# Gathering an attention chunk's loads into four transfers of ScalarE's queue, one step ahead

## The chip, the cores and the metric

The kernel runs on one core of a Trainium2 chip. Its time is the device time of one execution in microseconds (us), as the median of several runs.

## What is computed

One decoder block on 2048 positions of width 1024, in float32. A normalised input goes through one projection whose columns feed two mixers: a gated linear attention with four heads, and a gated short convolution. Their results go through an output projection, are added to the input, and a SwiGLU feed-forward block and a last norm follow. Cut to the part that matters here:

```python
h = rmsnorm(x, norm1_g)
p_q, p_k, p_v, p_g, p_a, c_b, c_c, c_h = split(h @ w_in)
log_a = log_sigmoid(p_a @ w_gate_up + b_gate) / 16
# per chunk: b = cumsum(log_a)
q_i, k_i, k_s = q * exp(b), k * exp(-b), k * exp(b_last - b)
o = tril(q_i @ k_i.T) @ v + q_i @ state
state = exp(b_last) * state + k_s.T @ v
o = rmsnorm(o, gla_norm_g) * silu(p_g)
```

## The kernel before

All wide products run as seven products of quarter matrices (PRODUCTS, a Strassen scheme), each of them as three matmuls of split operands (`product_step`, L323 to L330: high by high, high by low, low by high). A function `unit` (L332) does one such group: it loads raw weights, splits each quarter with ScalarE and VectorE into one of four `wq` buffers (`split`, L145 to L147), and runs the seven products, 12 matmuls each in the input projection. Between products results leave PSUM by a copy of ScalarE (L348) or an addition of VectorE (L352). The first product's bank is copied out before the third product goes on in the same bank.

The positions are worked through in two halves of two blocks of 512 (`in_proj`, L536). In each half the input projection has twelve units; the first six give k, q, v and the silu of g, and each result of 128 rows by 512 positions is stored to DRAM scratch: `s_kq` (four buffers a block), `s_v` and `s_g` (four each). The forget gate (L507) makes the cumulated decays and stores them to `s_d` (two buffers a block, L532). Every load and store goes through the helpers `load` (L138) and `store` (L141), both on the queue of SyncE, which issues in order.

The attention is background work. `gla_half` (L578) is a generator over eight chunks of 128 positions (two blocks of four), and `tick` (L187), called after each product, lets it go on by a step on every second call. The chunks of the first half run beside the units of both input projections, those of the second half beside the second input projection and the first output projection (L712). A chunk goes through four functions:

- `gla_load` (L603) takes four buffers of 128 by 4 by 128, issues 14 loads of 128 rows by 128 positions (four of k and q, two of the decays, four of v, four of g), and right behind them the two exponentials on ScalarE (L609, L610) and the two scalings of q and k on VectorE (L611, L612).
- `gla_scores` (L617) has TensorE form the scores (L622) and transpose k (L628) and v (L631); ScalarE copies the transposes back (L632, L633) and scales the carried state (L638).
- `gla_outputs` (L641) forms the outputs (L646, L648) and the chunk's state update (L653), and the sums of squares on ScalarE (L670).
- `gla_finish` (L678) transposes, multiplies by the gate and stores to `s_gla` (L686).

All buffers made by `bt` (L134) are of one pool of 11; there are four `wq` buffers, 28 operand pairs `op` and 8 PSUM banks. A scheduler orders each engine's instructions when the program is built, from its own estimate of their times; the engines then run their instructions in that order. Each DMA adds to one of eight completion semaphores, taken in turn, and waits, on the queue that issues it, for the DMA before it on the same semaphore.

The operand pairs of the second half are loaded (`load_pairs`, L476) while the first half's last unit runs: 28 transfers of 512 KB. Those of the output projection are loaded by `build_mix` (L706).

Of the kernel before, what the change touches and what calls it, by code (L numbers as in the profile page):

```python
# [10 lines left out]
F32 = mybir.dt.float32  # L11
# [7 lines left out]
P = 128  # L19
D = 1024  # L20
SEQ = 2048
PB = 512
NB = SEQ // PB
# [24 lines left out]
def tile_hymba_block(ctx, tc, x, xt, win, wa, wgu, wout, wffn, wdown, wdown_first, small, out):  # L48
    nc = tc.nc
    act, dve, pool, pe = nc.scalar, nc.vector, nc.gpsimd, nc.tensor  # L50

    def pool_of(name, bufs, **kw):
        return ctx.enter_context(tc.tile_pool(name=name, bufs=bufs, **kw))
# [8 lines left out]
    dram = pool_of("dram", 1, space=DRAM)  # L62
# [34 lines left out]
    def scratch(name, n):  # L97
        return [
            [dram.tile([P, PB], F32, name=f"{name}{b}_{i}") for i in range(n)] for b in range(NB)
        ]  # L100

    s_kq, s_d, s_v, s_g = scratch("sk", 4), scratch("sd", 2), scratch("sv", 4), scratch("sg", 4)
    s_x1 = scratch("sx", KD)
    s_mix = [[dram.tile([P, 2, PB], F32, name=f"sm{b}_{k}") for k in range(4)] for b in range(NB)]
    s_gla = [dram.tile([P, HEADS, 2, PB], F32, name=f"sgla{b}") for b in range(NB)]
# [19 lines left out]
    def col(c):  # L125
        return sml[:, c : c + 1]

    def bank(name="mm"):
        return ps.tile([P, PB], F32, name=name, tag="mm")

    def tt(name):
        return tp.tile([P, PB], F32, name=name, tag="t")

    def bt(name, shape=(P, PB)):  # L134
        return bx[0].tile(list(shape), F32, name=name, tag="b")

    def load(dst, src):
        return nc.sync.dma_start(dst, src)  # L138

    def store(dst, src):  # L140
        return nc.sync.dma_start(dst, src)  # L141
# [3 lines left out]
    def split(src, hi, lo):  # L145
        last_hi[:] = [act.activation(hi, src, AF.Copy)]  # L146
        return dve.tensor_tensor(lo, src, hi.bitcast(F32), ALU.subtract)  # L147
# [224 lines left out]
    def settled(c, in_psum):  # L372

        if not in_psum:
            return c
        s = tt("c11")
        act.activation(s[:], c[:], AF.Copy)
        return s
# [3 lines left out]
    def silu(c, in_psum):  # L382
        s = tt("sg") if in_psum else c
        last_silu[:] = [act.activation(s[:], c[:], AF.Silu)]
        return s
# [121 lines left out]
    def forget_gate(b, a_sb):  # L507
        em, dn, el = [
            mtiny.tile([P, 2, PT], F32, name=n, tag=n, bufs=4) for n in ("em", "dn", "el")
        ]  # L510
        for i in range(2):
            z = bank("z")
            pe.matmul(
                z[:], wgu_sb[0:64, i * P : (i + 1) * P], a_sb[0:64, :], start=True, stop=True
            )
            bg = col(C_BG + i)
            t1, t2 = bt("g1"), bt("g2")
            act.activation(t1[:], z[:], AF.Abs, bias=bg)
            dve.tensor_scalar(t2[:], z[:], bg, 0.0, ALU.add, ALU.min)
            act.activation(t1[:], t1[:], AF.Exp, scale=-1.0)  # L520
            act.activation(t1[:], t1[:], AF.Ln, bias=one_t)
            dve.tensor_tensor(t2[:], t2[:], t1[:], ALU.subtract)
            for t in range(PT):
                s = slice(t * P, (t + 1) * P)
                dve.tensor_tensor_scan(t1[:, s], ones[:], t2[:, s], 0.0, ALU.mult, ALU.add)
            bs = t1.rearrange("p (a b) -> p a b", b=P)
            dd = t2.rearrange("p (a b) -> p a b", b=P)
            act.activation(em[:, i, :], bs[:, :, 63], AF.Exp, scale=1.0 / 16.0)
            dve.tensor_tensor(dd, bs, bs[:, :, 63:64].to_broadcast([P, PT, P]), ALU.subtract)
            act.activation(el[:, i, :], dd[:, :, P - 1], AF.Exp, scale=1.0 / 16.0)  # L530
            dve.tensor_tensor(dn[:, i, :], em[:, i, :], el[:, i, :], ALU.mult)
            store(s_d[b][i][:], t2[:])  # L532
            yield
        decays[b] = em, dn, el

    def in_proj(half, ops, first):  # L536
        def units():
            for u in range(12):
                with ExitStack() as stack:
                    if half == 0 and u == 1:  # L540
                        stack.enter_context(tc.issue_after(last_load[0].ins))
                    yield first if u == 0 and first else unit(win[u], ops)

        units = units()
        for dst, i0 in ((s_kq, 0), (s_kq, 2), (s_v, 0), (s_v, 2)):
            for r, j, c, p in next(units):
                store(dst[2 * half + j][i0 + r][:], settled(c, p)[:])
        for i0 in (0, 2):
            for r, j, c, p in next(units):
                store(s_g[2 * half + j][i0 + r][:], silu(c, p)[:])  # L550
        background.append(gla_half(half))
        for i0 in (0, 2):
            cc = {(r, j): settled(c, p) for r, j, c, p in next(units)}
            ch = {(r, j): c for r, j, c, _ in next(units)}
            for r in range(2):
                i = i0 + r
                for j in range(2):
                    s = tp.tile([P, PB + 2], F32, name="u", tag="t")
                    dve.tensor_tensor(s[:, 2:], ch[r, j][:], cc[r, j][:], ALU.mult)
                    dve.tensor_copy(s[:, 0:2], halo[:, i, :])  # L560
                    dve.tensor_copy(halo[:, i, :], s[:, PB : PB + 2])
                    y = cc[r, j]
                    dve.tensor_scalar(y[:], s[:, 0:PB], col(C_CW + i), None, ALU.mult)
                    for n in (1, 2):
                        dve.scalar_tensor_tensor(
                            y[:], s[:, n : n + PB], col(C_CW + 4 * n + i), y[:], ALU.mult, ALU.add
                        )
            for r, j, c, _ in next(units):
                y = cc[r, j]
                dve.tensor_tensor(y[:], c[:], y[:], ALU.mult)  # L570
                hi = tp.tile([P, PB], F32R, name="hi", tag="t")
                split(y[:], hi[:], y[:].bitcast(F32R))
                dst = s_mix[2 * half + j][i0 + r]
                store(dst[:, 0, :], hi[:].bitcast(F32))
                store(dst[:, 1, :], y[:])


    def gla_half(half):  # L578
        chunks = [(b, t) for b in (2 * half, 2 * half + 1) for t in range(PT)]
        with tc.issue_after(last_silu[0].ins):  # L580
            tables = act.preload_act_table_set("natural_log_exp_and_others")
        with tc.issue_after(tables.ins):
            nxt = gla_load(*chunks[0])
        o = None
        for n, (b, t) in enumerate(chunks):
            cur = nxt
            s = gla_scores(b, t, *cur)
            yield
            if o is not None:
                gla_finish(*chunks[n - 1], *o)  # L590
                yield
            if n + 1 < len(chunks):
                nxt = gla_load(*chunks[n + 1])
            o = gla_outputs(b, t, *s)
            yield
        gla_finish(b, t, *o)
        done.add((b, t))
        yield
# [4 lines left out]
    def gla_load(b, t):  # L603
        s = slice(t * P, (t + 1) * P)
        kq, e, vt, g = [bt(n, (P, 4, P)) for n in ("kq", "ee", "vt", "gt")]
        for dst, src in ((kq, s_kq[b]), (e[:, 2:4, :], s_d[b]), (vt, s_v[b]), (g, s_g[b])):
            for i, r in enumerate(src):
                load(dst[:, i, :], r[:, s])
        act.activation(e[:, 0:2, :], e[:, 2:4, :], AF.Exp, scale=-1.0 / 16.0)  # L609
        act.activation(e[:, 2:4, :], e[:, 2:4, :], AF.Exp, scale=1.0 / 16.0)  # L610
        dve.tensor_tensor(kq[:, 0:2, :], kq[:, 0:2, :], e[:, 0:2, :], ALU.mult)  # L611
        dve.scalar_tensor_tensor(  # L612
            kq[:, 2:4, :], kq[:, 2:4, :], 0.125, e[:, 2:4, :], ALU.mult, ALU.mult
        )
        return kq, e, vt, g

    def gla_scores(b, t, kq, kt, v, g):  # L617
        sc = [ps.tile([P, 2, P], F32, name="sc", tag="mm") for _ in range(2)]
# [59 lines left out]
    def gla_finish(b, t, osb, g):  # L678

        ot = ps.tile([P, HEADS, P], F32, name="ot", tag="mm")  # L680
        for h in range(HEADS):
            pe.transpose(ot[:, h, :], osb[:, h, :], ident[:])
        dve.scalar_tensor_tensor(osb[:], ot[:], col(C_GN), g[:], ALU.mult, ALU.mult)
        split(osb[:], g[:].bitcast(F32R), osb[:].bitcast(F32R))
        for e, y in enumerate((g, osb)):
            store(s_gla[b][:, :, e, t * P : (t + 1) * P], y[:])  # L686
# [227 lines left out]
    def last_unit(src, ops, b12, y, ssq):  # L914
# [59 lines left out]
        [gate_weights(), gate(0, ops), row_stats(2), row_stats(3), unhurried(), h1_ahead()]  # L974
    )
    in_proj(0, ops, first)
    drain_background(lambda: len(background) < 2)
    ops = load_pairs(s_h1)
# [122 lines left out]
```

## Time and profile before

| | us |
|---|---|
| median of 3 runs | 2146.97 |
| lowest and highest run | 2140.72, 2151.3 |
| profiled execution | 2146.09 |
| its span, from the first to the last instruction | 2144.2 |
| TensorE matmul busy in the span | 2043.6 |
| VectorE, ScalarE, GpSimd busy | 1452.5, 1012.1, 997.0 |

The span is the part of the profiled execution that the trace covers. TensorE's matmuls overlap in the trace, and their ends are modelled, so a busy TensorE isn't TensorE at its best rate. DMA moves 467.64 MB in the span, 218 GB/s on average.

In the rows of the trace PE is TensorE, PEld its weight load, ACT ScalarE, DVE VectorE, POOL GpSimd and SP SyncE; a q behind the name is the engine's queue, where DMAs are issued. A row names the line, the operation and the tiles (out<-in, buffer numbers left out). An arrow in square brackets gives the idle time ahead of the instruction and what ended it.

### The profile page before, as it was taken

The page shows a single profiled execution, that of the slowest core. Times are in us where ns is not written, and L with a number is a line of the kernel's source. Part 1 is how long each engine was busy: PE and PEld are TensorE (multiplying, and loading weights), DVE is VectorE, ACT ScalarE, POOL GpSimd, SP SyncE. Part 2 cuts the span into 40 slices and gives each one's busy share as a digit, 9 for nine tenths or more (in the row PEclk, how much of TensorE's full clock was granted, in tenths as well). Part 3 has the DMA queues.
Part 4 walks back from the last instruction along what each step waited for, and adds up shares of the span by engine and source line. Part 5 has one row for each costly group of instructions (what it writes and reads, how often), then busy time and mean ns, then how long its engine had stood idle before and what let it go on. Part 6 is the DMA issues. An engine that isn't in the chain of part 4 may idle for free.

```text
span 2144.2 us, 26906 instructions
## 1 busy us (share of the span) xinstructions
PE 2043.6 (95%) x9133; PEld 1651.3 (77%) x9133; DVE 1452.5 (68%) x2034; ACT 1012.1 (47%) x1962; POOL 997.0 (46%) x714
## 2 busy tenths in 40 slices
PE   4899899999999999999999999999999999999996
PEld 2677687887888887788888887787888888887775
DVE  8849965556774486888887664554686677664554
ACT  4555434574544235555454553333454454553344
POOL 4526422122201274655655436774644654445774
PEclk9999999999999999999999999999999999999998
DMA  4259658532577884465464577689455455487662
GB/s 150 76 199 315 218 228 286 156 125 79 166 247 256 309 294 152 167 240 220 172 237 182 185 303 283 254 336 355 157 191 205 154 197 196 172 329 293 266 265 108
DMA packets 189977, 467.64 MB, mean 218 GB/s; under 512 B 19856, under 2 KB 65168, under 8 KB 180112
## 3 DMA queue, kind: packets, MB, share of 16 engines
q1 hardware_dynamic: 189840, 465.93, 59.9%
q8 instruction: 72, 1.18, 0.2%
q14 instruction: 65, 0.53, 0.1%
HBM read 297.03 MB, written 168.82 MB: 217 GB/s over the span
## 4 chain that ended last, share of the span: by engine, by line
PE 70%; DVE 11%; DMA 8%; issue 4%; ACT 3%; POOL 3%; SPq 1%; DVEq 0%; POOLq 0%; ACTq 0%
PE mm L328 20%; PE mm L330 20%; PE mm L329 19%; DVE wq L147 3%; PE mm L722 3%; PE mm L725 3%; PE mm L723 3%; DMA raw<-in_wdown_dram 2%; DVE h L440 2%; DMA raw<-in_wffn_dram 1%; DVE so L147 1%; DVE op L147 1%; DMA op<-shT 1%; DVE c L352 1%; ACT wq L146 1%
## 5 line engine op out<-in xcount | busy, mean ns | idle before, releaser
L328 PE MATMUL mm<-op,wq 128*128 128x512 f32 x2495 | 982.1, 395 | 33.0 <-ACT c L348 20.3
L330 PE MATMUL mm<-op,wq 128*128 128x512 f32 x2495 | 967.6, 392 | 12.4 <-DVE wq L147 11.2
L329 PE MATMUL mm<-op,wq 128*128 128x512 f32 x2495 | 975.6, 391 | 2.5 <-DVE op L147 2.5
L147 DVE TENSOR_TENSOR wq<-raw,wq 128x512 fp32r<-128x512 f32 (+2 forms) x628 | 536.6, 860 | 320.2 <-ACT wq L146 318.3
L146 ACT ACTIVATE wq<-raw 128x512 fp32r<-128x512 f32 (+2 forms) x628 | 367.1, 589 | 566.7 <-PE mm L330 415.4
L328 PEld LDWEIGHTS mm<-op,wq 128*128 128x128 f32 x2495 | 470.4, 189 | 152.1 <-ACT c L348 27.1
L330 PEld LDWEIGHTS mm<-op,wq 128*128 128x128 f32 x2495 | 470.5, 189 | 121.9 <-DVE wq L147 22.4
L329 PEld LDWEIGHTS mm<-op,wq 128*128 128x128 f32 x2495 | 470.7, 189 | 99.8 <-DVE op L147 3.0
L313 POOL TENSOR_TENSOR raw<-s,raw 128x512 f32<-128x512 f32 (+2 forms) x98 | 130.7, 1333 | 437.7 <-DVE wq L147 403.1
L352 DVE TENSOR_TENSOR c<-mm,c 128x512 f32<-128x512 f32 x270 | 185.1, 686 | 100.1 <-PE mm L330 98.0
L311 POOL TENSOR_TENSOR s<-raw 128x512 f32<-128x512 f32 (+2 forms) x98 | 130.8, 1335 | 207.9 <-DMA raw<-in_wffn_dram 96.1
L318 POOL TENSOR_TENSOR raw<-raw 128x512 f32<-128x512 f32 (+2 forms) x98 | 130.4, 1331 | 129.5 <-DVE wq L147 128.9
L348 ACT ACTIVATE c<-mm 128x512 f32<-128x512 f32 x270 | 156.4, 585 | 23.8 <-PE mm L330 23.0
L704 POOL TENSOR_TENSOR ssx<-ssx,q 128x512 f32<-128x512 f32 x52 | 75.2, 1459 | 151.0 <-ACT q L703 151.0
L312 POOL TENSOR_TENSOR raw<-raw 128x512 f32<-128x512 f32 (+2 forms) x98 | 137.2, 1400 | 4.6
L884 POOL TENSOR_TENSOR y<-c,y 128x512 f32<-128x512 f32 x66 | 98.6, 1496 | 67.3 <-DVE c L352 67.2
L147 DVE TENSOR_TENSOR so<-t,so 128x512 fp32r<-128x512 f32 x100 | 89.6, 902 | 23.8 <-ACT so L146 23.6
L722 PE MATMUL mm<-op,wq 128*128 128x512 f32 x256 | 100.9, 394 | 0.0
L723 PE MATMUL mm<-op,wq 128*128 128x512 f32 x256 | 99.7, 390 | 0.0
L146 ACT ACTIVATE wq<-s 128x512 fp32r<-128x512 f32 (+2 forms) x98 | 57.6, 588 | 89.2 <-PE mm L330 86.6
L147 DVE TENSOR_TENSOR wq<-s,wq 128x512 fp32r<-128x512 f32 (+2 forms) x98 | 81.9, 835 | 15.6 <-ACT wq L146 15.2
L146 ACT ACTIVATE so<-t 128x512 fp32r<-128x512 f32 x100 | 62.9, 630 | 48.6 <-DMA sa_B<-so 19.9
(177 smaller groups left out, 1931.2 us busy)
## 6 DMA issues: line engine op xcount, KB each, us to landing
raw<-in_wffn_dram SPq DMA_DIRECT2D x44, 1024.0 KB, 6.1
sa_T<-so SPq DMA_DIRECT2D x88, 512.0 KB, 4.9
op<-sa_T SPq DMA_DIRECT2D x88, 512.0 KB, 9.6
sa_B<-so SPq DMA_DIRECT2D x69, 512.0 KB, 3.4
op<-sa_B SPq DMA_DIRECT2D x69, 512.0 KB, 9.2
raw<-in_win_dram SPq DMA_DIRECT2D x24, 1024.0 KB, 5.7
raw<-in_wdown_dram SPq DMA_DIRECT2D x24, 768.0 KB, 6.1
sx<-y SPq DMA_DIRECT2D x48, 256.0 KB, 3.4
```

Of the source, the lines that this page charges most:

```text
L146: last_hi[:] = [act.activation(hi, src, AF.Copy)]
L147: return dve.tensor_tensor(lo, src, hi.bitcast(F32), ALU.subtract)
L311: pool.tensor_tensor(s1, a21, a22, ALU.add)
L312: pool.tensor_tensor(a21, a11, a21, ALU.subtract)
L313: pool.tensor_tensor(a11, s1, a11, ALU.subtract)
L328: pe.matmul(o[:], wh, xh, start=first and k == 0, stop=False, skip_group_check=True)
L329: pe.matmul(o[:], wh, xl, start=False, stop=False, skip_group_check=True)
L330: return pe.matmul(o[:], wl, xh, start=False, stop=k == n - 1, skip_group_check=True)
L348: act.activation(t[:], o[:], AF.Copy)
L352: dve.tensor_tensor(t[:], o[:], t[:], ALU.add)
L722: pe.matmul(o[e, j][:], wh, m[:, 0, :], start=k == 0, stop=False)
L723: pe.matmul(o[e, j][:], wh, m[:, 1, :], start=False, stop=False)
```

## The change

The four, two, four and four scratch buffers of a block become one buffer for each kind, with the rows side by side, and stores write one row of it. `gla_load` issues one transfer for each kind, on ScalarE's queue, the decays first. The exponentials and the scalings move to a function of their own, `gla_decay`. The loads of the next chunk are issued after the current chunk's scores, ahead of `gla_finish`, and `gla_decay` follows `gla_outputs`. Line numbers behind the first hunk grow by 4, from `gla_load` on by 7, and behind `gla_decay` by 8.

```diff
-    s_kq, s_d, s_v, s_g = scratch("sk", 4), scratch("sd", 2), scratch("sv", 4), scratch("sg", 4)
+    def gathered(name, n):
+        return [dram.tile([P, n, PB], F32, name=f"{name}{b}") for b in range(NB)]
+
+    s_kq, s_d = gathered("sk", 4), gathered("sd", 2)
+    s_v, s_g = gathered("sv", 4), gathered("sg", 4)
...
-            store(s_d[b][i][:], t2[:])
+            store(s_d[b][:, i, :], t2[:])
...
-                store(dst[2 * half + j][i0 + r][:], settled(c, p)[:])
+                store(dst[2 * half + j][:, i0 + r, :], settled(c, p)[:])
...
-                store(s_g[2 * half + j][i0 + r][:], silu(c, p)[:])
+                store(s_g[2 * half + j][:, i0 + r, :], silu(c, p)[:])
...
             nxt = gla_load(*chunks[0])
+            gla_decay(*nxt)
         o = None
         for n, (b, t) in enumerate(chunks):
             cur = nxt
             s = gla_scores(b, t, *cur)
             yield
+            if n + 1 < len(chunks):
+                nxt = gla_load(*chunks[n + 1])
             if o is not None:
                 gla_finish(*chunks[n - 1], *o)
                 yield
+            o = gla_outputs(b, t, *s)
             if n + 1 < len(chunks):
-                nxt = gla_load(*chunks[n + 1])
-            o = gla_outputs(b, t, *s)
+                gla_decay(*nxt)
             yield
...
-        for dst, src in ((kq, s_kq[b]), (e[:, 2:4, :], s_d[b]), (vt, s_v[b]), (g, s_g[b])):
-            for i, r in enumerate(src):
-                load(dst[:, i, :], r[:, s])
+        for dst, src in ((e[:, 2:4, :], s_d[b]), (kq, s_kq[b]), (vt, s_v[b]), (g, s_g[b])):
+            act.dma_start(dst[:], src[:, :, s])
+        return kq, e, vt, g
+
+    def gla_decay(kq, e, vt, g):
         act.activation(e[:, 0:2, :], e[:, 2:4, :], AF.Exp, scale=-1.0 / 16.0)
...
-        return kq, e, vt, g
```

In the built program 224 DMAs leave SyncE's queue (from 1233 in all) and 64 enter ScalarE's, which had none. The other engines keep their instructions, some of them in another order.

## Prediction

> **What bounds the kernel now.** I read the page first, then the sums over the stretch in which the attention chunks run, then the waits of TensorE (PE), and last, in order of time, the places of those waits. Page and stretch (columns of the second fence: busy us and number of instructions of each engine, granted clock of TensorE, DMA share, GB/s):
>
> ```profile
> span 2144.2 us, 26906 instructions
> PE 2043.6 (95%) x9133; PEld 1651.3 (77%) x9133; DVE 1452.5 (68%) x2034; ACT 1012.1 (47%) x1962; POOL 997.0 (46%) x714
> PE 70%; DVE 11%; DMA 8%; issue 4%; ACT 3%; POOL 3%; SPq 1%; DVEq 0%; POOLq 0%; ACTq 0%
> ```
> ```profile
> 237.00:705.00 468.00, 457.90 (x2322) 372.10 (x2321) 299.71 (x570) 228.50 (x541) 95.26 (x67) 0.99 0.57 191
> ```
> ```profile
> L138 SPq DMA_DIRECT2D kq<-sk x64: 319/430/1175, 237.2 to 660.5; - x64
> ```
>
> TensorE carries the chain of work that ends last (70%), and SyncE's queue 1% of it. The first load of a chunk goes out at 237.2 us and the last chunk's q and k at 660.5; their results are stored by 705. In those 468 us TensorE is busy for 457.90: at most 10.1 us of idle time can be won there, plus what the clock loses after it. ScalarE is busy for 228.50, so it has 239 us to spare, but it takes its instructions in order, and TensorE lives on its copies. The idle places of TensorE from 237 us on that touch a chunk, in order of time:
>
> ```profile
> 245.84 0.50 PE L328 MATMUL mm<-op,wq 128*128 128x512 f32 x1 [1.11 <-ACT c L348]
> 347.42 1.23 PE L622 MATMUL sc<-kq 64*128 64x128 f32 x8 [3.72 <-issue]
> 530.22 0.50 PE L328 MATMUL mm<-op,wq 128*128 128x512 f32 x1 [1.21 <-ACT c L348]
> 535.12 0.71 PE L622 MATMUL sc<-kq 64*128 64x128 f32 x8 [1.88 <-DVE kq L612]
> 655.09 0.71 PE L622 MATMUL sc<-kq 64*128 64x128 f32 x8 [0.35 <-PE mm L725]
> ```
>
> Three of the five are the scores (L622) waiting for q and k scaled by the decays. Their sum is 8.3 us. The second costs more than its 3.72, since the clock halves behind it:
>
> ```profile
> 340.00:343.00 3.00, 3.00 (x15) 2.49 (x14) 2.04 (x3) 0.63 (x1) 0.00 (x0) 1.00 0.87 300
> 347.50:353.50 6.00, 6.00 (x23) 5.00 (x24) 0.78 (x2) 0.98 (x2) 0.00 (x0) 0.50 0.94 247
> ```
>
> Six us at a clock of 0.50 are 3.0 us of lost work. So the place at 347 costs 6.7 us, and all five 11.3 us. That is the most that the change can win.
>
> **What the change does, part by part.** *The exponentials a step later.* Before, L609 follows its own loads at once, and ScalarE stands still for them:
>
> ```profile
> ACT ee L609 <- DMA ee<-sd: 22.7, 10, 4.9
> 238.85 0.64 ACT L146 ACTIVATE wq<-raw 128x512 fp32r<-128x512 f32 x1 [1.59 <-PE mm L330]
> 244.37 0.42 ACT L609 ACTIVATE ee<-ee 128x256 f32<-128x256 f32 x1 [4.88 <-DMA ee<-sd]
> ```
>
> At 245.84 that is why the PSUM copy (L348) is late. In the changed order L609 stands behind loads that go out before 238.85, so it runs at about 241 (the split at 238.85 and the issues ahead of it, priced below) and the copy is in time: -1.1. At 347 the exponentials stood behind a copy that itself waits for the end of the unit's last product:
>
> ```profile
> 343.74 0.60 ACT L377 ACTIVATE c<-mm 128x512 f32<-128x512 f32 x1 [2.02 <-PE mm L330]
> 344.76 0.41 ACT L609 ACTIVATE ee<-ee 128x256 f32<-128x256 f32 x1
> 345.20 0.42 ACT L610 ACTIVATE ee<-ee 128x256 f32<-128x256 f32 x1
> ```
>
> In the changed order L609 and L610 stand ahead of L377, one product earlier, so TensorE finds its scores ready: -3.7 and -3.0 of clock. At 655: -0.35. Late next there is the next matmul, which waits for nothing the trace shows.
>
> *The issues.* 14 loads a chunk, 224 in all, leave SyncE's queue; 4 a chunk, 64, enter ScalarE's. The nearest rows for one of the new shape (128 partitions by 4 rows of 128) are the stores to the chunk results, and below them the smaller loads (ns: least, median, most):
>
> ```profile
> L141 SPq DMA_DIRECT2D sgla<-gt x16: 513/525/1240, 344.0 to 699.9; - x16
> L138 SPq DMA_DIRECT2D ee<-sd x32: 319/400/449, 240.7 to 662.8; - x32
> ```
>
> I take 0.40 us for the decays and 0.52 for the other three, 2.0 us a chunk, 31 us in all, on ScalarE. The bounds for one are 0 (the issue runs beside the ACTIVATE ahead of it) and 1.24. ScalarE's 239 spare us cover the 31 in 13 of the 16 chunks, where the groups stand before a weight split (L146) that waits for TensorE anyway: 0, at most 26 us if the cover were gone. SyncE's relief is worth 0, because its queue is 1% of the chain. The 56 stores into the gathered buffers keep their size and rows, only the pitch in DRAM grows: 0, at most 0.2 us of SyncE each by the first row against 0.32.
>
> *The first chunks of the second half (524 to 535).* Here two groups of four issues, 8 in all, and a further L609 come ahead of one PSUM copy:
>
> ```profile
> 524.09 0.63 ACT L520 ACTIVATE g<-g 128x512 f32<-128x512 f32 x1
> 524.76 0.73 ACT L521 ACTIVATE g<-g,ones 128x512 f32<-128x512 f32 x1
> 526.33 0.64 ACT L146 ACTIVATE wq<-raw 128x512 fp32r<-128x512 f32 x1 [0.84 <-PE mm L330]
> 529.59 0.58 ACT L348 ACTIVATE c<-mm 128x512 f32<-128x512 f32 x1
> ```
>
> From the end of L520 at 524.7: two issues 0.9, L521 0.7, two issues 1.0, split 0.6, L609 0.4, two issues 0.9, L610 0.4, two issues 1.0, L609 0.4 (held a little until its load has landed), split 0.6, copy 0.6, which end at about 532.6 and not at 530.2. TensorE waits 2.4 longer there, and the 1.88 at 535 goes, because q and k are scaled during that wait: +0.5. With issues at nothing it would be -1; with the wait passing 3 us the clock may drop, as at 347, for 3.0 more.
>
> *The new waits.* This decides the forecast. In the built program each DMA adds to one of eight completion semaphores, taken in turn by both queues, and is issued only when the DMA before it on that semaphore has landed. On SyncE such a wait held only the queue. On ScalarE it holds splits and copies. Most of the 64 issues wait for DMAs that had landed long before. Two places are different: one between 612 and 640 (with the rivals), and the third chunk's first load. In the changed order it follows the L152 at 320.77, and its semaphore was last used by the load of the fourth B22 operand pair:
>
> ```profile
> 321.29 4.09 SPq L138 DMA_DIRECT2D op<-siB  x4
> op<-siB SPq DMA_DIRECT2D x4, 512.0 KB, 8.8
> 295.00:335.00 40.00, 40.00 (x212) 32.58 (x212) 32.14 (x55) 18.09 (x44) 8.89 (x8) 1.00 0.97 384
> ```
>
> That pair was the last of the four issues, at about 325.1, and landed 8.8 later, at 333.9. The 28 pairs of the second half fill the DMA engines (0.97 of them for 40 us), so the change doesn't bring it much earlier. Queued behind the held issue on ScalarE (copy L348 is the first product's, into the bank in which TensorE goes on at 329.15):
>
> ```profile
> 320.77 0.19 ACT L152 ACTIVATE hy<-hl 128x4 f32<-128x4 f32 x1
> 322.86 0.63 ACT L146 ACTIVATE wq<-raw 128x512 fp32r<-128x512 f32 x1 [1.91 <-PE mm L330]
> 325.93 0.64 ACT L146 ACTIVATE hi<-c 128x512 fp32r<-128x512 f32 x1 [2.44 <-DVE c L570]
> 326.47 0.37 ACT L632 ACTIVATE ee<-kt_ps 128x256 f32<-128x256 f32 x1
> 326.74 0.59 ACT L348 ACTIVATE c<-mm 128x512 f32<-128x512 f32 x1
> 328.92 0.39 PE L329 MATMUL mm<-op,wq 128*128 128x512 f32 x1
> 329.15 0.39 PE L328 MATMUL mm<-op,wq 128*128 128x512 f32 x1
> sm<-hi SPq DMA_DIRECT2D x1, 256.0 KB, 8.2
> ```
>
> From 333.9: issue 0.4, split 0.6 (334.9). The q and k load waits for a store issued at 327.0 that took 8.2 (335.2) and lasts 0.5 (335.7). Then L146, L632 and L348, 1.4 from the start of the first to the end of the third: 337.1. TensorE, which started the third product at 329.15, now starts it at 337.1: +8.0, and by the row of 347 the clock halves behind so long a wait: +3.0.
>
> The sum, against the profiled execution (2146.09 us, 1.9 of it outside its span of 2144.2; the median of the runs is 2146.97): -1.1 + 8.0 + 3.0 - 3.7 - 3.0 + 0.5 - 0.35 = +3.35, that is 2149.4 us.
>
> The Trainium skill, "TensorE: Matmul & The Clock Gate", Part 1, puts the half rate after an idle window of about 3.4 us and its end after about as long of work. The trace agrees that 3.72 us is enough, but its half rate lasts about 6 us. By the page's figure each of the two clock terms would be 1.7 (an estimate), and the sum would stay, since one comes and one goes.
>
> **The rivals.**
>
> *The holds don't reach TensorE, and the waits go.* For it: the loads ride a queue of their own, ScalarE is idle half of the stretch, and few of the 64 issues are held at all by the times of before. If the operand pair lands 8 us earlier, the copy is in time. Then -1.1 - 6.7 - 3.1 - 0.35 = -11.3, 2134.8; with the place at 524 unchanged 2138. Against it: the stretch before 335 is full of transfers that the change leaves alone.
>
> *ScalarE's issues land on the path (slower).* TensorE needs the first product's copy before its third product, one product (12 matmuls that start 0.23 us apart, as at 328.92 and 329.15, 2.7 us) after the first ends. A group of four issues is 2.0 us. From about 2.1 on (2.7 less the copy's 0.6) each group that stands ahead of a copy stops TensorE; at the row's 1.24 a group lasts 5.0 and gives 2.9 for each chunk in which it stands so. Four such chunks, the hold, and the dropped clock at 524: 3.35 + 11.6 + 3.0 = +18, 2164. Against it: in most chunks a split that waits for TensorE stands between. The loads of the output projection's operands and the stores beside them could hold ScalarE in the same way from 612 to 640 (one chunk's last load then waits for a pair issued at 613 and 10.4 us under way, until 623.4), but TensorE needs the next weights only at 628, and I take 0.
>
> ```profile
> op<-sm SPq DMA_DIRECT2D x1, 512.0 KB, 10.4
> 628.14 0.39 PE L722 MATMUL mm<-op,wq 128*128 128x512 f32 x1
> ```
>
> *It does nothing.* The chunks' loads were hidden, and the few waits only change place: 2146.1. The Trainium skill, "DMA: Bandwidth & Descriptors", section "Issuing engines are not separate DMA queues", says so in general: all issuing engines use the same 16 DMA engines, and starting transfers from several saves the issue time alone, usually small. The 1% of SyncE's queue in the chain agrees.
>
> **How the numbers follow.** The forecast has a chance of 0.50, with a range of its own from 2145 (the hold 4 us shorter) to 2155 (clock lost at 524, and 2 more for issues). The first rival has 0.17, the second 0.25, the last 0.08. The predicted time is 2149.4. The range of 8 in 10 reaches into both sides: 2137 to 2164. A measurement of this kernel can tell about 0.5% from no change, 10.7 us, which is nearly all that the first rival can win: faster 0.07. Slower needs over 2157: the second rival and a tail of the first case, 0.29. The rest, 0.64, lies between.
>
> **What would show it.** In the changed profile TensorE should stand at L328 near 329 for about 8 us, put down to ACT c L348, with the clock near 0.50 behind it, and ScalarE should show nothing between about 321 and 334. The wait of L622 near 347 should be gone, and L609's wait for its DMA should fall from 22.7 us to a few. If ScalarE runs through 321 to 334, the forecast is wrong towards faster; if L328 waits for ACT c L348 in many chunks, towards slower.

## The result and the profile after

The changed kernel takes 2161.5 us (median of 6 runs, 2157.36 to 2165.33), beside 2146.32 us for the kernel before in the same runs: a ratio of 1.0069, 95% interval 1.0053 to 1.0085. Timed a second time it took 2158.68 us, a ratio of 1.0067 (1.0049 to 1.0085). So it is slower, by 15.2 us in the first timing and 13.6 in the second (beside 2145.05). The forecast was 2149.4; the time lies in the range of 2137 to 2164, but above the likeliest case's own, which ended at 2155.

The page of the changed kernel (profiled execution 2162.86 us), with TensorE's share of the span and of the chain, and then three stretches of it (the columns are those shown of before; the last but two is the granted clock):

```profile
span 2161.1 us, 26659 instructions
PE 2053.9 (95%) x9133; PEld 1658.4 (77%) x9133; DVE 1452.8 (67%) x2034; ACT 1008.9 (47%) x1962; POOL 995.2 (46%) x714
PE 70%; DVE 12%; DMA 10%; issue 3%; ACT 3%; POOL 2%; SPq 0%; ACTq 0%; DVEq 0%; POOLq 0%
```
```profile
237.00:705.00 468.00, 451.06 (x2269) 365.89 (x2268) 299.07 (x566) 224.83 (x538) 96.20 (x67) 0.98 0.55 189
336.50:341.00 4.50, 4.50 (x12) 3.54 (x13) 1.89 (x3) 2.00 (x4) 0.00 (x0) 0.56 1.06 375
535.50:541.00 5.50, 5.47 (x21) 4.58 (x22) 5.50 (x13) 1.19 (x3) 0.00 (x0) 0.50 0.13 49
```

In the 468 us of the attention TensorE is busy for 451.1 and not for 457.9. No engine has more instructions in the span (compare the page of before); TensorE stands still for 7 us more. The second and third stretch show that its clock is about half behind two of the places where it stands (0.56 and 0.50); behind a third, at 634, it is too (0.52, shown at the end). Its waits in that stretch, and the wait of the exponentials for their load (engine, line, tile, what it waited for; us in total, times, longest):

```profile
PE mm L332 <- ACT c L352: 9.7, 3, 7.8
PE sc L630 <- DVE kq L621: 4.2, 1, 4.2
PE mm L332 <- DVE c L356: 2.9, 1, 2.9
ACT ee L618 <- DMA ee<-sd: 3.8, 2, 2.4
```

The scores' wait of 3.72 us near 347 is gone, and the exponentials wait 3.8 us for their loads and not 22.7. In their place stand three waits. The first is the hold that was forecast. In order of time, on the queues of SyncE (SPq) and ScalarE (ACTq), on ScalarE and on TensorE:

```profile
320.19 4.18 SPq L142 DMA_DIRECT2D op<-siB  x4
```
```profile
319.89 0.19 ACT L156 ACTIVATE hy<-hl 128x4 f32<-128x4 f32 x1
332.82 0.53 ACTq L614 DMA_DIRECT2D ee<-sd  x1
333.39 0.63 ACT L150 ACTIVATE wq<-raw 128x512 fp32r<-128x512 f32 x1 [13.31 <-DMA op<-siB]
334.99 0.63 ACT L150 ACTIVATE hi<-c 128x512 fp32r<-128x512 f32 x1 [0.97 <-DVE wq L151]
335.10 0.53 ACTq L614 DMA_DIRECT2D vt<-sv  x1
335.79 0.59 ACT L352 ACTIVATE c<-mm 128x512 f32<-128x512 f32 x1
```
```profile
336.43 0.79 PE L332 MATMUL mm<-op,wq 128*128 128x512 f32 x1 [7.76 <-ACT c L352]
```

ScalarE does nothing from 320.1 to 333.4. Its next instruction is the issue of a chunk's first load, and that issue stands for a DMA of another queue, the load of an operand pair: the last of the four siB loads goes out at 324.06 and is 8.7 us under way, so it lands at 332.8, where the issue starts. Behind it in ScalarE's queue is the PSUM copy that TensorE needs.

The second place (VectorE is DVE):

```profile
530.47 0.42 ACT L619 ACTIVATE ee<-ee 128x256 f32<-128x256 f32 x1 [0.40 <-ACT ee L618]
533.28 0.42 ACT L618 ACTIVATE ee<-ee 128x256 f32<-128x256 f32 x1 [2.39 <-DMA ee<-sd]
```
```profile
532.77 2.38 DVE L529 TENSOR_TENSOR_SCAN g<-ones,g 128x128 f32<-128x128 f32 x4
535.08 0.39 DVE L621 SCALAR_TENSOR_TENSOR kq<-kq,ee 128x256 f32<-128x256 f32 x1
```
```profile
535.52 1.23 PE L630 MATMUL sc<-kq 64*128 64x128 f32 x8 [4.21 <-DVE kq L621]
```

The factor for L621 is ready at 530.9 and its load of q and k has landed at 530.7, but L621 stands behind four scans of the forget gate in VectorE's queue, until 535.1. In the kernel before, the scaling (L612, 534.65) stood behind the same scans (530.13), but there TensorE had the 12 matmuls of one more product ahead of the scores; in the changed order the scores come first.

The third place:

```profile
618.32 6.13 SPq L142 DMA_DIRECT2D op<-sm  x5
```
```profile
621.37 0.58 ACT L352 ACTIVATE c<-mm 128x512 f32<-128x512 f32 x1
630.06 0.53 ACTq L614 DMA_DIRECT2D gt<-sg  x1
630.63 0.63 ACT L150 ACTIVATE wq<-raw 128x512 fp32r<-128x512 f32 x1 [8.68 <-DMA op<-sm]
```
```profile
631.30 0.69 DVE L151 TENSOR_TENSOR wq<-raw,wq 128x512 fp32r<-128x512 f32 x1 [6.78 <-ACT wq L150]
633.95 1.28 DVE L356 TENSOR_TENSOR c<-mm,c 128x512 f32<-128x512 f32 x2
```
```profile
634.69 0.80 PE L332 MATMUL mm<-op,wq 128*128 128x512 f32 x1 [2.88 <-DVE c L356]
```

Here ScalarE is held once more, by a load of the output projection's operands, which goes out at 619.02 and is 11.0 us under way. The held split (L150) holds VectorE, which takes its instructions in order too: the low part of that split (L151) stands ahead of the PSUM additions (L356), and for the first of these TensorE waits.

### The profile page after: what moved, and what is told of

Its sections match the earlier page's. It is cut to its first block, busy times and chain, and to the rows that moved or that the text cites. A ratio compares the mean times of both kernels' runs of the same rounds, so it can differ in the third digit from the quotient of the medians.

```text
span 2161.1 us, 26659 instructions
## 1 busy us (share of the span) xinstructions
PE 2053.9 (95%) x9133; PEld 1658.4 (77%) x9133; DVE 1452.8 (67%) x2034; ACT 1008.9 (47%) x1962; POOL 995.2 (46%) x714
## 4 chain that ended last, share of the span: by engine, by line
PE 70%; DVE 12%; DMA 10%; issue 3%; ACT 3%; POOL 2%; SPq 0%; ACTq 0%; DVEq 0%; POOLq 0%
PE mm L332 21%; PE mm L334 21%; PE mm L333 20%; DVE wq L151 3%; DVE h L444 2%; PE mm L730 2%; PE mm L733 2%; PE mm L731 2%; DMA raw<-in_wdown_dram 2%; DVE op L151 1%; DMA op<-shT 1%; DMA op<-sa_B 1%; DVE so L151 1%; DMA sx<-y 1%; DMA h<-sfT 1%
## 5 line engine op out<-in xcount | busy, mean ns | idle before, releaser
L151 DVE TENSOR_TENSOR wq<-raw,wq 128x512 fp32r<-128x512 f32 (+2 forms) x628 | 534.6, 857 | 330.6 <-ACT wq L150 327.9
L150 ACT ACTIVATE wq<-raw 128x512 fp32r<-128x512 f32 (+2 forms) x628 | 365.8, 587 | 590.0 <-PE mm L334 412.2
L356 DVE TENSOR_TENSOR c<-mm,c 128x512 f32<-128x512 f32 x270 | 184.9, 685 | 108.2 <-PE mm L334 105.9
L151 DVE TENSOR_TENSOR so<-t,so 128x512 fp32r<-128x512 f32 x100 | 89.9, 905 | 23.9 <-ACT so L150 23.8
L150 ACT ACTIVATE wq<-s 128x512 fp32r<-128x512 f32 (+2 forms) x98 | 57.4, 586 | 89.0 <-PE mm L334 84.1
L151 DVE TENSOR_TENSOR wq<-s,wq 128x512 fp32r<-128x512 f32 (+2 forms) x98 | 81.5, 832 | 17.6 <-ACT wq L150 17.1
L150 ACT ACTIVATE so<-t 128x512 fp32r<-128x512 f32 x100 | 62.6, 628 | 47.1 <-DMA sa_T<-so 19.6
```

Of the source, the lines that this page charges most:

```text
L356: dve.tensor_tensor(t[:], o[:], t[:], ALU.add)
```

## The experiments

To size each place, the same product matmuls of two traces were paired in order. The table gives how many us later than in the profile of before they start, ahead of and behind each place (the times on top are those of before, each number the median of five matmuls). Each row is one profiled execution. Chunks are named by their number among the 16; chunk 9 is the first of the second half.

| us later than before at | 328 | 345 | 360 | 523 | 546 | 622 | 650 | 705 | 2100 |
|---|---|---|---|---|---|---|---|---|---|
| changed kernel | -0.9 | 9.0 | 2.3 | 2.3 | 6.0 | 6.0 | 12.0 | 11.6 | 16.6 |
| changed kernel, second profile | -1.8 | 8.2 | 1.5 | 1.5 | 5.2 | 5.2 | 9.2 | 8.8 | 12.6 |
| old source order (e_early) | 0.3 | 10.5 | 3.8 | 3.8 | 6.1 | 6.1 | 8.6 | 8.1 | 11.8 |
| chunks 3, 14 on SyncE (e_mixed) | -2.9 | -2.9 | -1.5 | -1.5 | 0.9 | 0.9 | 1.8 | 1.3 | 4.0 |
| chunks 3, 4 on SyncE (e_s3) | -0.6 | -0.6 | -7.3 | -7.3 | -4.9 | -4.9 | -1.7 | -2.2 | 5.3 |
| chunks 9, 10 on SyncE (e_s9) | -2.4 | 7.6 | 0.9 | 0.9 | -0.6 | -0.6 | 2.3 | 1.8 | 4.7 |
| chunks 14, 15 on SyncE (e_s14) | -2.1 | 8.1 | 1.4 | 1.4 | 3.8 | 3.8 | 3.8 | 3.3 | 9.4 |
| these six on SyncE (e_few) | -0.9 | -0.9 | -7.5 | -7.4 | -7.3 | -7.3 | -7.3 | -7.8 | -4.3 |
| all on SyncE (e_sp) | -0.1 | -0.1 | -6.7 | -6.7 | -6.6 | -6.6 | -6.6 | -7.1 | -5.8 |
| all on SyncE, again (e_sp2) | -0.9 | -0.9 | -7.3 | -7.3 | -7.1 | -7.1 | -7.1 | -7.6 | -4.1 |

**All loads on SyncE's queue.** The edit to the changed kernel:

```diff
-            act.dma_start(dst[:], src[:, :, s])
+            load(dst[:], src[:, :, s])
```

> The changed kernel, with one thing undone: the 64 gathered transfers of the chunks go out on SyncE's queue and not on ScalarE's. First theory (ScalarE's queue is held by DMA issues that wait for other DMAs, near 321 to 333 and 622 to 630, and this reaches TensorE): the waits of L332 at 336 (7.76 us, with the clock behind it 11) and at 634 (5.7 with what stands around it) are gone, and the waits of the scores do not come back, because the decays' order comes from the gathered loads: 2161.5 - 11 - 5.7 = 2144.8, within 4. The 3.6 us lost at 524 to 540 may stay, since TensorE's order there is that of the changed kernel. Second theory (the issue time itself on ScalarE, some 31 us in all): gone too, the same time, so this run does not part the two. Third theory (the gathered buffers and the larger transfers are the cost): stays at 2161. Fourth (clock drops that come by chance): anywhere from 2150 to 2162, with no wait gone.

Measured: 2139.27 us (11 runs), a ratio to before of 0.9967 (0.9953 to 0.9982). TensorE's waits in the attention, and the exponentials near 342 on ScalarE:

```profile
PE mm L332 <- ACT c L352: 2.5, 2, 1.3
PE sc L630 <- DVE kq L621: 1.9, 1, 1.9
```
```profile
341.54 0.40 ACT L618 ACTIVATE ee<-ee 128x256 f32<-128x256 f32 x1
343.66 0.60 ACT L381 ACTIVATE c<-mm 128x512 f32<-128x512 f32 x1 [1.27 <-PE mm L334]
```

All three places are gone. The time lies 5.5 us below the 2144.8 that was expected, outside its 4 us. The place at 347, which cost before 6.7 us, stays gone: the exponentials still stand ahead of L381, the copy that waits for the product. So the gathered buffers and larger transfers aren't the cost; this version is faster than both kernels, than the one before by 0.3%. I had left 3.6 us at 524 as possible; they went too (-6.7 to -6.6).

**Two held chunks on SyncE's queue.** Chunks 3 and 14 alone:

```diff
-            act.dma_start(dst[:], src[:, :, s])
+            if (b, t) in ((0, 2), (3, 1)):
+                load(dst[:], src[:, :, s])
+            else:
+                act.dma_start(dst[:], src[:, :, s])
```

> The changed kernel, but the loads of only two of the 16 chunks, the third and the fourteenth, go out on SyncE's queue: the two groups whose issues were held on ScalarE. 56 of the 64 issues stay on ScalarE. First theory (the holds): nearly the time of the run with all loads on SyncE, 2145, within 4, with no wait of TensorE for ScalarE's copy near 336 and none for VectorE's addition near 634. Second theory (issue time on ScalarE): 8 of 64 issues gone are an eighth of the loss of 15, 2159.6. Third theory (buffers and larger transfers): 2161.5.

Measured: 2153.97 us, 1.0032 (1.0020 to 1.0044): between the first theory's 2145 and the 2159.6 and 2161.5 of the others, so that no theory had it. The waits near 336 and 634 are gone, but ScalarE's hold moved on to chunk 4 (line numbers behind the load grow by 3 in the runs with this edit):

```profile
341.40 0.53 ACTq L617 DMA_DIRECT2D ee<-sd  x1
344.19 0.63 ACT L150 ACTIVATE wq<-raw 128x512 fp32r<-128x512 f32 x1 [8.20 <-DMA sm<-c]
345.15 0.42 ACT L622 ACTIVATE ee<-ee 128x256 f32<-128x256 f32 x1
```
```profile
346.31 1.22 PE L633 MATMUL sc<-kq 64*128 64x128 f32 x8 [5.55 <-issue]
```

Chunk 4's first load waits for a store (sm<-c) to land, and now chunk 4's own scores come late. In the changed kernel TensorE was already 9 us late there and didn't feel it. The first theory's mechanism holds; that moving one group is enough was wrong.

**The place near 336 with both groups moved, and the other two places alone.** The same edit with chunks 3 and 4:

> The changed kernel, with only the third and fourth chunks' loads on SyncE's queue. First theory: the place 329 to 350 costs 9.1 us, by the offsets of equal matmuls between the traces of the changed kernel and of the one with all loads on SyncE. With the changed kernel at 2158.7 (the middle of the two times of its order) 2149.6, within 3; no wait of L332 near 336 and none of the scores near 347; the waits near 535 and 634 stay. Second theory (issue time): 8 of 64 issues of a loss of 22: 2156. If the hold only moves on to the scores, as with the third chunk alone: 2154.

Measured: 2150.67 us, 1.0024 (1.0011 to 1.0037), where 2149.6 was expected. In the table the step from 328 to 345 falls from 9.9 to 0, the step of -6.7 behind it stays, and the other two waits stay, 4.2 and 2.9 us. They cost less than in the changed kernel, 2.4 and 3.2: behind the second the clock doesn't drop this time.

With chunks 9 and 10:

> The changed kernel, with only the first two chunks of the second half loaded by SyncE's queue. Theory of the issues (eight issues, some 5 us of ScalarE's queue, push the exponentials and so the scaling of q and k behind four scans of VectorE): the wait of the scores near 535 falls from 4.2 to about 1.9 us and the half clock behind it goes: -3.6 against the changed kernel, 2155 from 2158.7. Rival (the moved order of TensorE, the scores ahead of a product, makes the wait): 4.2 us stay, 2158.7. The waits near 336 and 634 stay in both.

Measured: 2153.92 us, 1.0037 (1.0024 to 1.0051), where 2155 was expected. TensorE's waits:

```profile
PE mm L332 <- ACT c L352: 7.2, 1, 7.2
PE mm L332 <- DVE c L356: 2.6, 1, 2.6
PE sc L633 <- DVE kq L624: 1.9, 1, 1.9
```

```profile
531.31 0.41 DVE L624 SCALAR_TENSOR_TENSOR kq<-kq,ee 128x256 f32<-128x256 f32 x1
531.64 2.40 DVE L529 TENSOR_TENSOR_SCAN g<-ones,g 128x128 f32<-128x128 f32 x4
```

The wait of the scores is back at 1.9: without the eight issues the scaling of q and k (L624 here) stands ahead of the four scans in VectorE's queue. TensorE's order is that of the changed kernel but for one place (8 of 9133 matmul records), so the scores' earlier place alone doesn't make the wait; it takes VectorE's order too.

With chunks 14 and 15:

> The changed kernel, with only the fourteenth and fifteenth chunks' loads on SyncE's queue. First theory (ScalarE's queue held until a load of the output projection's operands lands, passed on by VectorE's order): the wait of L332 for VectorE's addition near 634 is gone, 5.9 us by the offsets between traces: 2152.8 from the changed kernel's 2158.7, within 3. The waits near 336 and 535 stay. Second theory (issue time on ScalarE): 8 of 64 issues of 22 us: 2156.

Measured: 2155.78 us, 1.0037 (1.0023 to 1.0051). The time is that of the second theory (2156) and at the edge of the first one's (2152.8 within 3), so it doesn't part them. The trace does: the step from 622 to 650 is 0 where the changed kernel has 6.0 and 4.0, and only the other two waits are left.

**Six chunks on SyncE's queue, ten on ScalarE's.** The same edit with chunks 3, 4, 9, 10, 14 and 15:

> The changed kernel, with the loads of six of the 16 chunks on SyncE's queue: the third and fourth, the first two of the second half, and the fourteenth and fifteenth. The other ten chunks, 40 of the 64 issues, stay on ScalarE. First theory (the loss of 22 us against all loads on SyncE lies at three places, 329 to 350, 524 to 548 and 622 to 644, and elsewhere an issue on ScalarE costs nothing): 2139 to 2143, none of the three waits left. Second theory (issue time on ScalarE): 40 of 64 issues keep 40/64 of the 22: 2153. A hold that only moves to a neighbour, as with two chunks, would show as a new long idle time of ScalarE ahead of a split, put down to a DMA.

Measured: 2141.72 us, 0.9985 (0.9972 to 0.9999). TensorE's waits in the attention:

```profile
PE sc L633 <- DVE kq L624: 1.9, 1, 1.9
PE mm L332 <- ACT c L352: 1.2, 1, 1.2
```

With 40 of the 64 issues still on ScalarE the traces lie within 1 us of those with all on SyncE, up to 705. An issue of 0.53 to 0.66 us that nobody waits behind costs nothing that the trace shows up to there. The median is 2.4 us above that of all on SyncE, with intervals that overlap, and 3.6 above that of its second timing (below), with intervals that just don't, so a cost of some 2 to 4 us isn't ruled out. The second theory wanted 2153.

**The changed kernel again.**

> The changed kernel itself, unchanged, timed beside the other runs of this group, with a second profile. First theory (the loss comes from waits that the order of the queues makes each time): 2156 to 2162, between the two times seen for this order (2161.5, and 2156.0 with one pair of splits swapped), and the same waits: L332 7.8 us near 336, L630 4.2 near 535, L332 2 to 3 near 634. Rival (chance): the waits or their places differ from the first profile. In the feed-forward part, behind 820 us, the kernels with loads on ScalarE's queue lost 3.5 to 4.8 us in three of three profiles and the others 0 in two of two; if that is chance, it may be absent here.

Measured: 2158.68 us. The waits came again at the same three places: 8.0, 4.2 and 2.4 us.

**The source order.** First the steps of the loop as before, with the four transfers on ScalarE's queue; then the kernel before with the new steps and its own 14 loads:

```diff
             s = gla_scores(b, t, *cur)
             yield
-            if n + 1 < len(chunks):
-                nxt = gla_load(*chunks[n + 1])
             if o is not None:
                 gla_finish(*chunks[n - 1], *o)
                 yield
+            if n + 1 < len(chunks):
+                nxt = gla_load(*chunks[n + 1])
+                gla_decay(*nxt)
             o = gla_outputs(b, t, *s)
-            if n + 1 < len(chunks):
-                gla_decay(*nxt)
```

> The changed kernel, with the source order of the steps undone: loads and decays of the next chunk stand together behind the finish of the last one, as in the kernel before; the four transfers stay on ScalarE's queue. In the built program only one pair of ScalarE's splits is swapped, because the order comes from the scheduler's estimates. First theory (the order in the source decides nothing; queue and shape of the transfers do): the same as the changed kernel, 2161.5 within 3, with the same waits at 336 and 634 and none at 347. Rival (the later decays win the wait at 347): that wait comes back with its clock, 2168.

> The kernel before, with only the source order changed as in the change: loads one step ahead, decays a step later; separate buffers and 14 loads a chunk on SyncE's queue stay. First theory (the order in the source decides little, for the scheduler puts the instructions of TensorE, GpSimd, ScalarE and VectorE where they were but for three of them): the time of before, 2146.3 within 2, and the scores' wait of 3.72 us at 347 stands. Rival (the later decays alone win): the wait at 347 and its clock are gone, 2139.6.

Measured: 2156.01 us, 1.0043 (1.0027 to 1.0060), with the three waits as in the changed kernel and none near 347 (5.5 us below the 2161.5 expected, outside its 3; the interval of the changed kernel's second timing, 1.0049 to 1.0085, overlaps); and 2147.66 us, 0.9994 (0.9981 to 1.0006), with the scores' wait of before:

```profile
PE sc L627 <- issue: 3.7, 1, 3.7
```

So "one step ahead" and "a step behind" in the source do nothing that shows by themselves: the scheduler orders each engine's instructions from its own estimates. With the four gathered transfers of the change on SyncE's or ScalarE's queue it puts the exponentials ahead of the copy; with the 14 loads of before it doesn't, in either source order. With the gathered loads on SyncE the two source orders give the same order of instructions.

The change also puts the decays' load ahead of that of q and k, and no run parts this from the gathering. In programs that were built and not timed, either is enough: the kernel before with only the decays' loads put first, 14 as they were, has the exponentials ahead of that copy, and so has the version with the four transfers on SyncE's queue when q and k go first. What the order alone would win is open.

**Another engine's queue.** All 64 transfers on GpSimd's:

```diff
-            act.dma_start(dst[:], src[:, :, s])
+            pool.dma_start(dst[:], src[:, :, s])
```

> The changed kernel, with the 64 gathered transfers on GpSimd's queue. In the built program the DMAs of that queue count on eight completion semaphores of their own, so that an issue there waits for other chunk loads and for its buffer, but not for SyncE's operand loads and stores. First theory (the shared semaphores make the holds): no engine stands for a load or store of another queue, the waits near 336 and 634 are gone, and the time is that of SyncE's queue, 2139 to 2145, the wait near 535 at 1.9 or gone. Rival (any queue of an engine that computes is held): GpSimd's sums of the weights (L315 to L322) come late, TensorE waits for splits of wq, 2150 to 2160.

Measured: 2156.33 us, 1.0038 (1.0023 to 1.0052); the first theory's time (2139 to 2145) failed, and the time lies in the rival's range (2150 to 2160), but not for its reason. The waits near 336 and 634 are gone, as the first theory has it, but the order changed and brought others: 2.4 us near 254 for a split of wq (it stands on ScalarE behind a split that waits 4.3 us for VectorE, not for GpSimd's sums), 3.0 for operand pairs near 346 and 349, and the scores again, for the exponentials stand behind the copy as before:

```profile
PE sc L630 <- issue: 3.7, 1, 3.7
PE mm L332 <- DMA op<-siT: 3.0, 2, 2.0
PE mm L332 <- ACT wq L150: 2.4, 1, 2.4
```
```profile
351.74 0.60 ACT L381 ACTIVATE c<-mm 128x512 f32<-128x512 f32 x1 [6.93 <-PE mm L334]
352.75 0.41 ACT L618 ACTIVATE ee<-ee 128x256 f32<-128x256 f32 x1
```

So the gathered transfers don't always move the exponentials, and this run doesn't tell cleanly what semaphores of its own are worth.

**Many more issues on ScalarE.** Separate buffers, all 14 loads a chunk on ScalarE's queue:

```diff
-                load(dst[:, i, :], r[:, s])
+                act.dma_start(dst[:, i, :], r[:, s])
```

> Separate buffers as before and 14 loads a chunk, all on ScalarE's queue, 224 issues in place of 64, source order as in the changed kernel. First theory: a group of 14 issues lasts 7.4 us at 0.53 each, the ninth also waits for the landing of the first on its semaphore; a group longer than 2.1 us ahead of a copy stops TensorE, so that most of the 16 chunks lose some 5 us and part of the clock behind it: 2230, at least 2180, with TensorE waiting for ScalarE's copies in most chunks. Rival (ScalarE's spare time hides issues of any number): 224 issues are 119 us of 239 spare us, the time stays near the changed kernel's, under 2165.

Measured: 2181.76 us, 1.0158 (1.0139 to 1.0177): just above the first theory's least (2180), far below its 2230 and far above the rival's 2165. Against the same source with its 14 loads on SyncE's queue (2147.66, above) the change of queue costs some 34 us. The issues' times in ns (least, median, most), and TensorE's largest waits:

```profile
L611 ACTq DMA_DIRECT2D kq<-sk x64: 326/442/1276, 233.5 to 684.6; - x64
```
```profile
PE mm L328 <- ACT c L348: 18.4, 5, 7.8
PE mm L727 <- ACT wq L146: 6.5, 1, 6.5
PE sc L627 <- issue: 5.1, 1, 5.1
```

224 issues of some 0.44 us are about 98 us of ScalarE, and TensorE waits for ScalarE in a handful of places, one of them again a wait of 7.8 near 335. Neither "most chunks" nor "hidden at any number" is right.

**All on SyncE's queue again.**

> All 64 gathered transfers on SyncE's queue once more, unchanged, beside the other kernels of this group: 2139.3 within 2.5, and below the kernel before. The second profile shows whether the part behind 705 us, in which kernels with loads on ScalarE's queue ended 2 to 7 us later against the profile of before, stays near 0 (it was 0.7).

Measured: 2138.14 us, 0.9952 (0.9937 to 0.9967). Up to 705 the trace repeats the first one within 1 us. Behind 705 it loses 3.5 us against the profile of before, as the changed kernels do (5.0 and 3.8), so that loss isn't tied to ScalarE's queue. One place of it, a matmul behind the same idle time in the runs e_sp and e_sp2, which are the same program, and e_few:

```profile
885.40 0.50 PE L334 MATMUL mm<-op,wq 128*128 128x512 f32 x1 [3.26 <-DVE wq L151]
```
```profile
883.11 0.80 PE L334 MATMUL mm<-op,wq 128*128 128x512 f32 x1 [3.25 <-DVE wq L151]
```
```profile
885.70 0.80 PE L334 MATMUL mm<-op,wq 128*128 128x512 f32 x1 [3.26 <-DVE wq L151]
```

After 3.25 to 3.26 us of idle time the first matmul takes 0.50 us in one execution and 0.80 in two others; the granted clock over the next 3.6 us is 1.00 in the first and 0.57 and 0.54 in the others. All 14 profiles have this idle time. In ten of them the clock drops behind it and they lose 1.3 to 2.9 us there against the profile of before; in that of before, e_sp, e_s9 and e_ahead it doesn't, and they lose nothing there. So part of the loss behind 705 is a clock that drops in some executions and not in others of one program. The part behind 705 has no instruction of the change; the rest of the loss there, and why the drop came in most of these profiles, isn't settled.

## Why the prediction held, and where it failed

- **The hold at 329** (+8.0, clock +3.0): right. The wait is 7.76 and 8.0 us, the place costs 9.9 and 10.0 with its clock, whose share is thus about 2 and not 3. It was found by asking, for each new issue, what its semaphore counted last.
- **The wait at 347 with its clock** (-3.7 - 3.0): right in size, -6.4 to -6.7 in every kernel with the exponentials ahead of the copy but e_mixed, where a hold took its place. The reason given, that the exponentials stand a step later in the source, was wrong: the gathered transfers with the decays first move them, in either source order (e_ahead, e_early, e_sp), through the scheduler's estimates. That the size came out is in part luck.
- **The place at 245** (-1.1) and **655** (-0.35): the sizes are about right, -0.9 and -0.6 from the start of the stretch to 328, and -0.4 from 650 to 705. But the first is won where it was forecast in the second profile alone: the wait at 245, 1.11 us before, is 0.98 and 0.38 in the two profiles of the changed kernel, and in the first of them a wait near 266 fell in its place, from 1.72 to 1.00.
- **The place at 524** (+0.5): the step failed. I kept TensorE's old order and let the scores find q and k scaled "during that wait". The scores came first in TensorE's order, the scaling stayed behind four scans in VectorE's, and the wait grew to 4.2 with half the clock behind it: +3.7 in both profiles. That the clock might drop there was named, for 3.0 more, but not put into the sum.
- **"TensorE needs the next weights only at 628, and I take 0"**, on 612 to 640: the step failed. The hold itself was named, with its transfer. That it reaches TensorE through VectorE, in whose queue a split of the held weights stands ahead of the PSUM additions, was not followed: +6.0 and +4.0, of which the wait itself is 2.9 and 2.4 and the rest the half clock behind it. With a wait of 2.9 and no drop of the clock the place costs 3.2 (e_s3). Setting ScalarE's hold against TensorE's need of weights left out a third queue.
- **The issues** at 0 where covered: right in effect (e_few), though one takes 0.53 to 0.64 us and not 0.40 to 0.52.
- **The rivals.** The first, the waits go and no hold reaches TensorE, is what the loads on SyncE's queue do: 2139.27 and 2138.14 against its 2134.8 to 2138. The second, the issues land on the path, is not what made most of the loss (e_few); at 524 it has a part, for there, with eight issues fewer on ScalarE, the scheduler puts the scaling ahead of the scans, and the place goes from +3.7 to -1.5 (e_s9). The third, nothing happens, is out. The page of the Trainium skill "DMA: Bandwidth & Descriptors", section "Issuing engines are not separate DMA queues", says that starting transfers from several engines saves the issue time alone. Here the queue of the loads mattered by some 20 us (2158.68 against 2138.14 to 2139.27), most of it through what stands behind a waiting issue.

The terms up to 705 were forecast at +3.35 and measured at +11.6 and +10.0 (from the matmul ahead of 237 on). The difference is the two failed steps, 9.2 and 7.2 us above their terms, less about 1 for the hold's clock. Another 5.0 and 3.8 us lie behind 705, where nothing was forecast. That the time still lies within 2137 to 2164 is partly luck: the upper end was priced for another cause, four chunks stopped by the length of their issues.

## What to carry to other kernels

A DMA issued from an engine that computes is an instruction of that engine's queue: its half microsecond mostly hides (40 such issues here cost nothing that the trace shows in their stretch), but it may stand for another queue's transfer through a shared completion semaphore, and then everything behind it stands too, on that engine and on each engine whose own queue waits for it. So look up, for each issue, which DMA its semaphore counted last and when that lands, and follow the hold through every in-order queue up to the engine that bounds the kernel. Take apart a change that gathers, moves and changes queues: here the gathered transfers, decays first, won 7 to 9 us on SyncE's queue, the moves in the source did nothing that shows, and ScalarE's queue lost about 20.

## What the runs showed of the hardware beyond that

TensorE's half clock came behind idle times of 3.72 us in the kernel before and of 2.88 and 2.38 in the two profiles of the changed one (near 634). The stretch behind 634.69 in the first is

```profile
634.70:641.00 6.30, 6.30 (x15) 4.96 (x16) 6.30 (x15) 3.62 (x14) 0.00 (x0) 0.52 1.04 398
```

and in the second the clock is 0.57 from 633.3 to 637. But 2.88 us at the same place of e_s3 left it at 1.00 over the next 4.2 us, and 3.25 to 3.26 us were followed by either rate in one program. The Trainium skill, "TensorE: Matmul & The Clock Gate", Part 1, says that the gate watches a free-running window of about 3.4 us, so that the point of the change varies from execution to execution; the two outcomes of e_sp and e_sp2 agree with that. The 2.88 and 2.38 us are shorter than the page's idle window, so here it isn't a lower bound. And issues on ScalarE's queue run partly beside its ACTIVATEs: the issue at 335.10 starts 0.11 us after the split at 334.99 that takes 0.63.
